# Input projection and first MLP matrix: the order of the last five products of a group

## The chip, the cores and the metric

The kernel runs on one core of a Trainium2 chip. The metric is the device time of one execution in microseconds (us), lower is better. The core's engines work side by side and wait for each other by semaphores: TensorE (PE, matmuls; PEld is its weight loading), VectorE (DVE), ScalarE (ACT), GpSimd (POOL) and SyncE (SP), which here only issues loads and stores. Matmuls write into PSUM, eight banks of 128 x 512 fp32; everything else lies in SBUF.

## The reference

One layer of a decoder trunk over 512 tokens of width 2048, in fp32:

```python
h = rmsnorm(x, g_mix[l])
z = jnp.einsum('bsd,dc->bsc', h, w_in[l])          # input projection, 10248 columns
cb, cc, cv, q, k, v, f_logit, gate_c, gate_a = jnp.split(z, SPLIT_POINTS, axis=-1)
...                                                # gated conv, forgetting attention, merge
x = x + jnp.einsum('bsd,de->bse', merged, w_mix_out[l])
h = rmsnorm(x, g_mlp[l])
u = jnp.square(jax.nn.relu(jnp.einsum('bsd,df->bsf', h, w_ff1[l])))   # first MLP matrix
x = x + jnp.einsum('bsf,fd->bsd', u, w_ff2[l])
...
return rmsnorm(x, g_final)
```

The change touches how the products with `w_in` and `w_ff1` are computed, and nothing of what they are.

## The kernel before

**Precision.** An fp32 operand is split in two: `split` (L100, L101) lets ACT write a rounded high half `hi` and DVE the rest, `lo`. A product is then hi·hi + hi·lo + lo·hi, three matmuls. The split weights lie in tiles th and tl, two buffers of each; so the split of a product can begin when the matmuls of the product before the last have read theirs.

**Seven products for eight.** Each group of columns of `w_in` or `w_ff1` is a two by two matrix of weight blocks X[i, j] (i: half of the rows, taken in steps of two; j: which of two column ranges). The tokens and rows on the activation side form a two by two matrix too, A11, A12, A21, A22. Instead of eight block products a group runs seven (Strassen's scheme in Winograd's form), with sums on both sides. On the activation side the sums S1 to S4 are made once per stage, already split (the tiles named A, S or ST). On the weight side they are made for each group, in place, by DVE (`sub`, L104):

- X00 becomes X01 - X00 (the first sum), used with S1
- X01 becomes X11 - X01 (the second), used with S3
- X11 becomes X11 - new X00 (the third), used with S2; the old X11 is used with S4
- X10 becomes X10 - new X11 (the fourth), used with A22

**A group.** `Group.head` loads X00 and X10 and runs A11 into bank a and A12 into bank b; `Group.tail` loads X01 and X11 (and X00 and X10 again if they were given up) and runs the other five. Bank a collects A11, S2 and S1, with a snapshot to SBUF by ACT after each (`snap`, L200). Bank c takes S4 alone, bank d S3 and then A22, with a snapshot of d between. Outputs leave through `put(i, j, ...)`: (0, 0) is a's first snapshot plus b; (1, 1) is the snapshot of d plus the last one of a; (0, 1) is the last snapshot of a plus c, read from the bank by `plus` (L217 where it is scaled, else L107); (1, 0) is a's second snapshot plus d. Each weight block lies in one of four slots (x0 to x3); `done` puts a slot at the end of the list `free`, and the next load takes the first of it, in the order X00, X10, X01, X11. SP issues the loads in this order, and a load waits until the slot's last reader is through.

A product of a group of width 256 (`mm_cols`, L139, L141 for the high half of the weights, L143 for the low half) has 48 matmuls of 128 x 256. Group gV0 and gV1 go through `mm_rows` (L156, L157, L159).

**The groups.** Input projection: gV0 and four groups `kq` run all their heads first and then all their tails, one tail behind the other; then gV1, six groups of conv columns and eight of gate columns follow whole, a head and then its tail (`whole`). Ahead of each of the first four conv groups, two heads of attention stand in the source. First MLP matrix (`ff1`): sixteen groups, of which 0 and 1 run head, head, tail, tail, and the others whole. The banks (a, b, c, d) of the heads held back are 6 for c and 7 for d in gV0 and all four kq groups, with a different a for each; c is bank 1 in all of ff1 but its last group, and bank 0 in the conv and gate groups.

In some groups (`apart`) S4 has two more small matmuls into a spare bank (L588): one conv group, three gate groups, and groups 2, 6, 10 and 14 of ff1.

**After ff1's outputs.** `put_u` applies a ReLU (L861), squares (L833, L838), makes sums of the four blocks of u for the next stage (into r, L850 for its low half) and stores high and low half to `s_d` by POOL's queue (L852, L853). The sums for j = 1 are made as soon as (0, 1) and (1, 1) are put; those for j = 0 wait in the list `later` until the next group's tail has taken its snapshot after S2.

**What sets the order.** The source's order is a priority: a planner walks it with its own costs, and on each engine takes the first instruction that it holds ready. So the order on an engine can differ from the source's where something is not ready, on DVE and ACT above all, and now and then on PE.

The stage after the input projection is `gemm_t` (L301), in the same banks; the one after ff1 is `unit`, whose banks come from a new pool, of which `a` overlaps banks 0 and 1 of the old.

Of the kernel before, what the change touches and what calls it, by code (L numbers as in the profile page):

```python
# [45 lines left out]
def tile_hybrid_block(ctx: ExitStack, tc, x, g_mix, w_in, b_f, b_gate, conv_w, w_conv_out,  # L46
# [56 lines left out]
    def sub(out, a, b):  # L103
        nc.vector.tensor_tensor(out=out, in0=a, in1=b, op=ALU.subtract)  # L104

    def add(out, a, b):
        nc.vector.tensor_tensor(out=out, in0=a, in1=b, op=ALU.add)  # L107
# [60 lines left out]
    class Group:  # L168
# [69 lines left out]
        def tail(self):  # L238
            if self.at:
                X = self.X  # L240
            else:
                X = {(i, 0): self.load(i, 0) for i in range(2)}
            X[0, 1], X[1, 1] = self.load(0, 1), self.load(1, 1)
            a = self.a
            c = self.acc("c")
            self.run(c, "S4", X[1, 1], True)
            sub(X[0, 0], X[0, 1], X[0, 0])
            sub(X[0, 1], X[1, 1], X[0, 1])
            sub(X[1, 1], X[1, 1], X[0, 0])
            self.run(a, "S2", X[1, 1], False)  # L250
            sub(X[1, 0], X[1, 0], X[1, 1])
            self.done(1, 1)
            s2 = self.snap(a)
            while later:
                later.pop(0)()
            d = self.acc("d")
            self.run(d, "S3", X[0, 1], True)
            self.done(0, 1)
            d1 = self.snap(d, self.scale)
            self.run(a, "S1", X[0, 0], False)  # L260
            self.done(0, 0)
            s4 = self.snap(a, self.scale)
            add(d1, d1, s4)
            self.put(1, 1, d1)
            self.plus(s4, c, self.scale)
            self.put(0, 1, s4)
            self.run(d, "A22", X[1, 0], False)
            self.done(1, 0)
            self.plus(s2, d)
            self.put(1, 0, s2)  # L270


    def eights(t, w=S):
# [804 lines left out]
```

## Time and profile before

| What | Value |
|---|---|
| Median of three runs | 2507.99 us (2504.74 to 2508.36) |
| The profiled execution, time | 2509.61 us |
| The profiled execution, span | 2507.9 us |
| Mean granted clock of TensorE | 0.996 |
| Weight loads of PE (PEld) | 90% of the span |
| DMA | 465.06 MB, mean 185 GB/s |

How to read it. The span is the time from the first to the last instruction of one profiled execution. In a timeline a row is start (us from the span's start), length (us), engine, line, operation, the tile written and the tiles read, and shapes; in brackets the idle time of the engine just before it and what ended it. In a view of waits a row is who waited for whom, then us in total, times, and the longest. In a view of windows a row is the stretch, its length, the busy time of PE, PEld, DVE, ACT and POOL with the number of instructions, the granted clock of PE, the busy share of the DMA engines and GB/s. Matmuls are pipelined: 0.28 us long, they start every 0.11 us or so, so the distance of starts tells the pace, not the length.

### The profile page before, as it was taken

To read this page: it belongs to the slowest core of one execution; us is meant where nothing else is said; L and a number is where in the kernel's file an instruction comes from. 1 tells how busy PE (TensorE), PEld (TensorE's weight loads), DVE (VectorE), ACT (ScalarE), POOL (GpSimd) and SP (SyncE) were. 2 spreads that over 40 slices of the span, in tenths; PEclk is the share of its full clock that TensorE was granted. 3 is DMA by queue.
4 is the path that set the end of the run, shared out by engine and by line. 5 is a ranking of instruction groups with operands and counts; after the bars stand their busy time and mean duration, and the time that the engine had idled before them with its cause. 6 is when DMAs were issued, how large, how long until landed. Compare 5 with 4: busy or idle time off the path is not lost. (4 is left out here: it accounts for less than half of the span.)

```text
span 2507.9 us, 39017 instructions
## 1 busy us (share of the span) xinstructions
PE 2453.0 (98%) x16911; PEld 2255.6 (90%) x16911; DVE 1902.2 (76%) x1498; ACT 1149.7 (46%) x1136; POOL 112.4 (4%) x184
## 2 busy tenths in 40 slices
PE   8999999999999999999999999999999999999997
PEld 7999989999999988888889999999998878787785
DVE  7877677789767744435678888898887877878888
ACT  6443434334444622235556666666664333333343
POOL 0000000000000000000000000000011000000010
PEclk9999999999999999999999999999999999999999
DMA  7554444456543554435654655646688557665573
GB/s 242 163 174 156 155 133 147 139 180 207 165 137 120 190 173 137 146 133 201 202 170 181 223 182 197 242 172 217 219 307 282 162 190 238 214 213 158 187 257 107
DMA packets 289919, 465.06 MB, mean 185 GB/s; under 512 B 10236, under 2 KB 194644, under 8 KB 289620
## 3 DMA queue, kind: packets, MB, share of 16 engines
q1 hardware_dynamic: 260704, 330.40, 41.2%
q0 software_dynamic: 28176, 131.08, 14.0%
q8 instruction: 132, 2.16, 0.4%
q10 hardware_dynamic: 868, 1.10, 0.1%
q14 instruction: 39, 0.32, 0.0%
HBM read 370.26 MB, written 92.27 MB: 184 GB/s over the span
## 5 line engine op out<-in xcount | busy, mean ns | idle before, releaser
L101 DVE TENSOR_TENSOR tl<-x,th 128x2048 fp32r<-128x2048 f32 (+1 forms) x252 | 574.7, 2288 | 216.6 <-ACT th L100 198.7
L100 ACT ACTIVATE th<-x 128x2048 fp32r<-128x2048 f32 (+1 forms) x252 | 482.4, 1917 | 498.5 <-PE a L141 184.8
L104 DVE TENSOR_TENSOR x<-x,x 128x2048 f32<-128x2048 f32 (+1 forms) x144 | 329.2, 2286 | 14.8 <-DMA x<-in_w_in_dram 7.1
L100 ACT ACTIVATE th<-y 128x2048 fp32r<-128x2048 f32 x80 | 153.7, 1921 | 271.3 <-DVE y L104 102.6
L101 DVE TENSOR_TENSOR tl<-y,th 128x2048 fp32r<-128x2048 f32 x80 | 182.8, 2284 | 47.3 <-ACT th L100 47.3
L101 DVE TENSOR_TENSOR tl<-raw,th 128x2048 fp32r<-128x2048 f32 x40 | 91.7, 2292 | 152.0 <-ACT th L100 151.5
L156 PE MATMUL a<-th,us 128*128 128x512 f32 x512 | 200.9, 392 | 3.0 <-ACT o L861 1.5
L157 PE MATMUL a<-th,us 128*128 128x512 f32 x512 | 199.4, 389 | 0.0
L139 PE MATMUL a<-ST,th 128*128 128x256 f32 x768 | 181.6, 281 | 5.9 <-ACT th L100 5.9
L141 PE MATMUL a<-ST,th 128*128 128x256 f32 x768 | 181.1, 280 | 0.0
L100 ACT ACTIVATE th<-raw 128x2048 fp32r<-128x2048 f32 x40 | 76.7, 1918 | 175.5 <-PE pt L302 62.6
L139 PEld LDWEIGHTS a<-ST,th 128*128 128x128 f32 x768 | 146.5, 191 | 6.6 <-ACT th L100 6.5
L141 PEld LDWEIGHTS a<-ST,th 128*128 128x128 f32 x768 | 146.5, 191 | 0.0
L139 PE MATMUL a<-S,th 128*128 128x256 f32 x576 | 134.1, 278 | 5.5 <-ACT th L100 5.5
L159 PE MATMUL a<-tl,us 128*128 128x512 f32 x512 | 136.9, 389 | 0.1
L141 PE MATMUL a<-S,th 128*128 128x256 f32 x576 | 133.5, 277 | 0.0
L156 PEld LDWEIGHTS a<-th,us 128*128 128x128 f32 x512 | 96.1, 188 | 28.5 <-ACT th L100 6.1
L139 PE MATMUL d<-ST,th 128*128 128x256 f32 x512 | 119.1, 278 | 0.0
L141 PE MATMUL d<-ST,th 128*128 128x256 f32 x512 | 119.1, 278 | 0.0
L159 PEld LDWEIGHTS a<-tl,us 128*128 128x128 f32 x512 | 96.0, 188 | 20.7 <-DVE tl L101 0.9
L139 PEld LDWEIGHTS a<-S,th 128*128 128x128 f32 x576 | 108.2, 188 | 6.8 <-ACT th L100 6.5
L157 PEld LDWEIGHTS a<-th,us 128*128 128x128 f32 x512 | 96.1, 188 | 19.6
(284 smaller groups left out, 6237.6 us busy)
## 6 DMA issues: line engine op xcount, KB each, us to landing
x<-in_w_in_dram SPq DMA_DIRECT2D x86, 1024.0 KB, 5.9
x<-in_w_ff_dram SPq DMA_DIRECT2D x66, 1024.0 KB, 7.8
y<-in_w_ff_dram SPq DMA_DIRECT2D x64, 1024.0 KB, 6.2
us<-s_d POOLq DMA_DIRECT2D x48, 1024.0 KB, 8.9
s_d<-rh POOLq DMA_DIRECT2D x32, 896.0 KB, 5.0
s_d<-r POOLq DMA_DIRECT2D x32, 896.0 KB, 8.2
raw<-in_w_mix_out_dram SPq DMA_DIRECT2D x24, 1024.0 KB, 5.1
g_d<-o SPq DMA_DIRECT2D x32, 256.0 KB, 2.2
```

Source lines behind the costliest of these rows:

```text
L100: nc.scalar.activation(out=hi, in_=src, func=AF.Copy)
L101: nc.vector.tensor_tensor(out=lo, in0=src, in1=hi.bitcast(F32), op=ALU.subtract)
L104: nc.vector.tensor_tensor(out=out, in0=a, in1=b, op=ALU.subtract)
L139: nc.tensor.matmul(o, hi[:, q, js], Sh, start=first and q == 0 and j == 0, stop=False, skip_group_check=True)
L141: nc.tensor.matmul(o, hi[:, q, js], Sl, start=False, stop=False, skip_group_check=True)
L156: nc.tensor.matmul(o, Sh, hi[:, q, :], start=begin and q == 0, stop=False, skip_group_check=True)
L157: nc.tensor.matmul(o, Sl, hi[:, q, :], start=False, stop=False, skip_group_check=True)
L159: nc.tensor.matmul(o, Sh, lo[:, q, :], start=False, stop=q == nq - 1, skip_group_check=True)
```

## The change

The five products of `Group.tail` run in the order S4, S3, S2, A22, S1 instead of S4, S2, S3, S1, A22. The first sum of weights stands ahead of S4, the second between S4 and S3, the third between S3 and S2, the fourth between S2 and A22. The snapshots, the calls of `done`, and the puts move with their products: the slots are given up in the order X01, X11, X10, X00 (before: X11, X01, X00, X10), and output (1, 0) is put ahead of (1, 1) and (0, 1). No instruction is added or removed.

```diff
             a = self.a
+            sub(X[0, 0], X[0, 1], X[0, 0])
             c = self.acc("c")
             self.run(c, "S4", X[1, 1], True)
-            sub(X[0, 0], X[0, 1], X[0, 0])
             sub(X[0, 1], X[1, 1], X[0, 1])
+            d = self.acc("d")
+            self.run(d, "S3", X[0, 1], True)
+            self.done(0, 1)
             sub(X[1, 1], X[1, 1], X[0, 0])
+            d1 = self.snap(d, self.scale)
             self.run(a, "S2", X[1, 1], False)
             sub(X[1, 0], X[1, 0], X[1, 1])
             self.done(1, 1)
             s2 = self.snap(a)
             while later:
                 later.pop(0)()
-            d = self.acc("d")
-            self.run(d, "S3", X[0, 1], True)
-            self.done(0, 1)
-            d1 = self.snap(d, self.scale)
+            self.run(d, "A22", X[1, 0], False)
+            self.done(1, 0)
             self.run(a, "S1", X[0, 0], False)
             self.done(0, 0)
+            self.plus(s2, d)
+            self.put(1, 0, s2)
             s4 = self.snap(a, self.scale)
             add(d1, d1, s4)
             self.put(1, 1, d1)
             self.plus(s4, c, self.scale)
             self.put(0, 1, s4)
-            self.run(d, "A22", X[1, 0], False)
-            self.done(1, 0)
-            self.plus(s2, d)
-            self.put(1, 0, s2)
```

## The prediction

> **What bounds the kernel now.** I read the page first, then the waits of TensorE, then the timelines around those waits.
>
> ```profile
> span 2507.9 us, 39017 instructions
> PE 2453.0 (98%) x16911; PEld 2255.6 (90%) x16911; DVE 1902.2 (76%) x1498; ACT 1149.7 (46%) x1136; POOL 112.4 (4%) x184
> ```
>
> TensorE (PE) is busy for 98% of the span, and the change removes none of its products. So it can only alter two things: how long PE stands still, and how fast it steps while it runs. The waits of PE, whole execution (us in total, times, longest):
>
> ```profile
> PE a L139 <- ACT th L100: 11.4, 8, 2.8
> PE d L156 <- ACT th L100: 8.1, 14, 3.7
> ...
> PE a L156 <- ACT o L861: 1.5, 1, 1.5
> PE a L156 <- ACT th L100: 0.8, 1, 0.8
> ...
> PE pt L301 <- DVE o L107: 0.4, 1, 0.4
> ```
>
> The d L156 row belongs to the last stage (`unit`), which is not touched. The eight waits of "a L139" and the one of "a L156" on th are all of one kind: the product that writes bank a behind one that writes bank c, which is S2 behind S4. Around one such group of the input projection (start us, length us):
>
> ```profile
> 140.69 0.28 PE L139 MATMUL d<-A,th 128*128 128x256 f32 x1
> 146.13 0.28 PE L139 MATMUL c<-S,th 128*128 128x256 f32 x1
> 152.66 0.39 PE L139 MATMUL a<-S,th 128*128 128x256 f32 x1 [0.92 <-ACT th L100]
> 152.88 0.28 PE L141 MATMUL a<-S,th 128*128 128x256 f32 x1
> ```
> ```profile
> 139.21 2.29 DVE L104 TENSOR_TENSOR x<-x,x 128x2048 f32<-128x2048 f32 x1 [1.33 <-DMA x<-in_w_in_dram]
> 141.53 0.69 DVE L107 TENSOR_TENSOR o<-o 128x512 f32<-128x512 f32 x1
> 142.25 0.69 DVE L217 SCALAR_TENSOR_TENSOR o<-c,o 128x512 f32<-128x512 f32 x1
> 143.28 2.29 DVE L104 TENSOR_TENSOR x<-x,x 128x2048 f32<-128x2048 f32 x1 [0.34 <-DMA x<-in_w_in_dram]
> 145.49 2.28 DVE L101 TENSOR_TENSOR tl<-x,th 128x2048 fp32r<-128x2048 f32 x1
> 147.69 0.68 DVE L107 TENSOR_TENSOR o<-d,o 128x512 f32<-128x512 f32 x1
> 148.29 4.61 DVE L104 TENSOR_TENSOR x<-x,x 128x2048 f32<-128x2048 f32 x2
> 152.82 2.29 DVE L101 TENSOR_TENSOR tl<-x,th 128x2048 fp32r<-128x2048 f32 x1
> ```
> ```profile
> 140.90 0.60 ACT L200 ACTIVATE o<-a 128x512 f32<-128x512 f32 x1 [4.84 <-PE a L143]
> 143.34 1.92 ACT L100 ACTIVATE th<-x 128x2048 fp32r<-128x2048 f32 x1 [1.84 <-DMA x<-in_w_in_dram]
> ```
>
> One product takes 5.44 us (140.69 to 146.13). S4's weights, the last of four loads, land at 143.3. From there VectorE (DVE) does the second sum, the low half of S4, a sum into an output, and only at 148.29 the third sum, on which S2 depends; ScalarE (ACT) then needs 1.92 us for S2's high half. S2 was due at 151.57 and starts at 152.66, 1.09 late. The rows of DVE also show that the first sum (139.21) stands ahead of S4's split (145.49) already, though the source has it behind: the planner starts what is ready. That part of the edit I cost at nothing, since the sum waits for its load either way.
>
> In most later groups of `ff1` the same chain just fits:
>
> ```profile
> 1723.34 1.93 ACT L100 ACTIVATE th<-x 128x2048 fp32r<-128x2048 f32 x1 [4.64 <-DVE x L104]
> 1726.29 0.28 PE L139 MATMUL a<-ST,th 128*128 128x256 f32 x1
> ```
>
> S2's high half is there at 1725.27 and S2 starts at 1726.29: 1.0 us to spare, PE never idle. Those groups have nothing to give.
>
> **What the waits cost beyond their length.** The longest one leaves a mark behind it:
>
> ```profile
> 1294.94 0.58 PE L139 MATMUL a<-ST,th 128*128 128x256 f32 x1 [2.85 <-ACT th L100]
> ...
> 1299.17 0.41 PE L141 MATMUL a<-ST,th 128*128 128x256 f32 x1
> 1299.38 0.41 PE L139 MATMUL a<-ST,th 128*128 128x256 f32 x1
> ...
> 1300.87 0.31 PE L141 MATMUL a<-ST,th 128*128 128x256 f32 x1
> ...
> 1338.95 0.38 PE L139 MATMUL a<-ST,th 128*128 128x256 f32 x1 [1.46 <-ACT th L100]
> ```
> ```profile
> 1286.00:1302.00 16.00, 13.15 (x91) 12.95 (x91) 15.43 (x12) 8.59 (x11) 1.15 (x2) 0.79 0.37 138
> ...
> 1342.00:1490.00 148.00, 148.00 (x1259) 148.00 (x1258) 125.63 (x96) 91.74 (x92) 7.99 (x15) 1.00 0.59 201
> 1500.00:1640.00 140.00, 140.00 (x1238) 140.00 (x1237) 120.80 (x93) 88.68 (x89) 7.45 (x14) 1.00 0.61 212
> ```
>
> After 2.85 us of idle the matmuls start 0.21 us apart instead of 0.113 until 1300.87, and the granted clock of that stretch is 0.79. The other two window rows show a second effect: PE is "busy" all the time in both, yet it starts a matmul every 117.6 ns in the first (148/1259) and every 113.1 ns in the second (140/1238), at the same granted clock. The slow stretch lies behind the restart at 1338.95, after 1.46 us of idle that left the clock at 1.00; it ends between 1490 and 1500, where group 6 runs its spare products (L588).
>
> **The change part by part.**
>
> 1. *S3 goes ahead of S2.* S3 needs the second sum only, S2 the third, A22 the fourth: one sum of 2.29 us per product of 5.44 us, instead of three ahead of one product. With the rows above, S3's high half can follow the second sum at 145.49 and be done at 147.5, against 151.57 when it is due: 4 us to spare. S2 then gets 5.44 us more. I take all nine waits as gone: 11.4 + 0.8 = 12.2 us idle. Each restart costs 0.28 on top: 1.09 late with 0.92 idle is 0.17, and the first step of 0.22 (152.66 to 152.88) is 0.11 over the normal one; nine times, 2.5. The slow clock behind the 2.85 wait: 5.93 us at 0.213 in place of 0.113 per step, 2.8. Together **-17.5 us**; bounds 0 and -17.5.
>
> 2. *The step of PE.* With no restart at 1338.95, group 2's own spare products should leave the fast step on: 1259 matmuls by 4.5 ns, **-5.6 us**. No row shows what a restart decides, so the bounds are 0 and -5.6.
>
> 3. *S1 goes last, so bank c comes free late.* c is read by L217 (`plus(s4, c)`), behind the snapshot of a after S1 and the add into d1. Before, S1 was followed by A22, 5.44 us of cover. Now the last product's end starts that chain, and where the next product is S4 of another group it must not write c before. This holds where tails follow tails: four boundaries among gV0 and the four kq groups (bank 6 for all), one between the two held heads of `ff1` (bank 1). Elsewhere two products of the next head lie between. The chain, by the rows: 140.90 to 142.94, 2.1 us, with both engines free. They may not be: DVE can be in S4's low half (145.49 to 147.69) and ACT in S3's high half; then the add starts about 148.0 and the bank is free near 149.4, 3.1 us idle. It can also be nothing, where PE has S3's matmuls to run meanwhile. Bounds 0 and 3.1 per boundary; I take 2.1, the chain as the trace shows it, plus 0.28: five times 2.4, **+11.9 us**. Behind PE nothing else queues there that is not waiting for PE itself.
>
> 4. *Ends of the two stages.* The hand-over to the last stage waits for the last reader of any bank:
>
> ```profile
> 1863.64 0.68 DVE L107 TENSOR_TENSOR o<-d,o 128x512 f32<-128x512 f32 x1
> ...
> 1864.42 0.47 PE L156 MATMUL a<-th,us 128*128 128x512 f32 x1 [1.47 <-ACT o L861]
> ```
>
> The wait is put down to an ACT row, but it ends 0.1 us behind the read of d (1863.64 + 0.68). That read has one link behind the last product; S1's has three, 2.1 us and up to 4.3 with a 2.28 sum in flight: +0.5 to +2.9, taken 1.5. The hand-over to `gemm_t` (0.4 idle now) has the same three links, but four banks to begin with: 0 to +1.7, taken 0.5. And the squares' sums of the last group (four adds of 0.42, one of 2.02: 3.7 us on DVE) move into the first unit: 0 to +3.7, taken 0.6. **+2.6 us**.
>
> 5. *Taken at nothing.* Bank d: its two uses and the snapshot between them keep one whole product of cover (S2 for S1), as has a (A22 for S3). The weight buffers are freed after the fourth to seventh product as before, so the SP queue's loads are issued at the same places; the stores of an output pair trade places. In `ff1` the pair of u-sums moves one product later, out of the last product into the head, with its two stores on POOL's queue and the reuse of r; their readers come a stage later. What hides this is DVE's slack (120.8 us busy of 140). If that cover were gone, ACT would wait for r with the next high half behind it; the bound is the 1.0 us to spare now, in 14 groups: 14 us. I exclude most of it because S2 no longer needs three sums early.
>
> Sum: -17.5 - 5.6 + 11.9 + 2.6 = **-8.6 us**, on the profiled execution's 2509.6 (span 2507.9) gives 2501.0. That execution lies 1.6 above the median of the runs, 2508.0; from the median the sum gives 2499.4. I say 2500.
>
> **Rivals.**
>
> *A, the step stays slow.* Only part 2 fails, because another restart (or none at all) leaves PE at 117.6 ns. For it: nothing in the trace says what picks the step, and the five new restarts are chances for the wrong one. Against: the group quoted at 140 steps at 113 ns (5.44 us for 48 matmuls) though waits of this kind stand in the groups around it. 2508.0 - 3.0 = 2505: within 0.2%.
>
> *B, bank c ends on the other side.* The chain of part 3, at the five boundaries, with busy engines: 3.1 us idle. That passes the 2.85 us after which the clock was seen to fall, so each boundary would cost 3.1 + 0.28 + 2.8 = 6.2, together 31; with part 2 lost as well, -17.5 + 31 + 2.6 = +16, 2524; with it, 2518. It decides from (17.5 + 5.6 - 2.6)/5 = 4.1 us per boundary, which an idle of 2.85 with its slow clock (5.9) exceeds and one of 2.1 does not. For it: the DVE and ACT rows at 145.5 fall just there. Against: waits of 1.5 us left the clock alone. The Trainium skill (TensorE: Matmul & The Clock Gate, "HAM oscillation") says that a gap over about 3.4 us puts the array back to half clock, by a window that runs freely; this trace shows it after 2.85, so the measurement is the stricter. By the page's figure B would need longer waits than I find.
>
> *C, PE fills the wait.* The planner puts S3's matmuls ahead of S4's, as it starts whatever is ready; part 3 falls to about 0.5 per boundary, 2.5 in all: -18.0, 2490. For it: the first sum standing ahead of S4's split is such a move. Against: S3's high half is itself only ready 1.3 us after the boundary (147.5 against 146.13).
>
> *D, the change doesn't do what it says.* If the planner's order of sums and splits were the same after it, the nine waits would stay and only parts of 3 appear: 2508, no change. Against: products write banks in source order, and the waits of step 1 hang on that order.
>
> **How the numbers follow.** Forecast 0.40, A 0.15, B 0.24, C 0.14, D 0.07. About 0.2%, 5 us, is what a measurement of this kernel can tell from no change. Faster by more: forecast and C, 0.54. Within: A and D, 0.22. Slower by more: B, 0.24. The range reaches down to C (2489) and up into B, to 2517, where some boundaries but not all trip the clock; the upper half of B and little else, about 0.15, is left out. The likeliest case has its own range, 2495 to 2504, from part 3 at 1.4 to 3.0 per boundary.
>
> **What would show it.** Step 1: no wait of "a" on th behind c, and S3 behind S4 with its high half early. Step 2: 1238 matmuls or so per 140 us right after group 2. Step 3: new waits of "c" on DVE's L217 or L107 at five places, about 2.1 us each, with the granted clock at 1.00 around them. Step 4: a wait of 2 to 4 us at the hand-over to the last stage. Step 5: no new wait in the groups of 1500 to 1860. I would be wrong if the waits at bank c were long enough to slow the clock, or if the groups that had none before got some.

## The result, and the profile after

The change makes the kernel slower: 2530.64 us median of six runs (2525.25 to 2535.30) beside 2508.18 of the kernel before on the same chip (2504.41 to 2511.37), a ratio of 1.0087, 95% interval 1.0072 to 1.0103. The prediction said 2500 with a range up to 2517; the time lies outside it, on the other side.

The head of the page after, then the waits of TensorE in the whole execution (us in total, times, longest):

```profile
span 2528.3 us, 39053 instructions
PE 2454.6 (97%) x16911; PEld 2251.9 (89%) x16911; DVE 1908.1 (75%) x1498; ACT 1150.5 (46%) x1136; POOL 112.6 (4%) x184
```
```profile
PE d L143 <- DVE tl L101: 20.7, 14, 2.4
PE d L156 <- ACT th L100: 8.7, 15, 3.7
PE d L139 <- ACT th L100: 8.3, 5, 2.5
...
PE d L159 <- DVE tl L101: 2.1, 2, 1.9
```

Each engine has as many instructions as before; the 36 more in the total of the head are none of theirs. The 1.6 us more of busy PE is noise beside a span 20.4 longer: PE stands still. The nine waits ahead of S2 are gone (the one wait of bank a on a split that is left, 0.7 us at 1316.66, is A11 of group 2 in ff1). In their place stand three kinds. Fourteen times the second half of S3 (L143, low half of the weights) waits for DVE's `split`: 20.7 us. Five times S3's first half waits for its high half: 8.3 us. And in the last stage two products wait for their low halves, 1.9 and 0.2 us.

The first matmul of each stage in the timeline of PE gives the length of the stages in the two profiled executions (us, one start less the other):

| Stage | before | after | difference |
|---|---|---|---|
| the five tails behind each other, to gV1 | 144.31 | 147.19 | +2.9 |
| gV1, conv and gate groups, to gemm_t | 645.88 | 644.25 | -1.6 |
| gemm_t to ff1 | 354.63 | 354.86 | +0.2 |
| ff1, groups 0 and 1 | 88.07 | 82.98 | -5.1 |
| ff1, group 2 to the last stage | 544.08 | 563.08 | +19.0 |
| last stage, to the end of PE | 630.59 | 635.83 | +5.2 |

So the loss is in ff1 from group 2 on, where the prediction had expected no new wait. One of these groups after, VectorE first, then the matmul that waits:

```profile
1717.06 2.29 DVE L104 TENSOR_TENSOR x<-x,x 128x2048 f32<-128x2048 f32 x1 [0.23 <-DMA x<-in_w_ff_dram]
1723.03 2.29 DVE L104 TENSOR_TENSOR x<-x,x 128x2048 f32<-128x2048 f32 x1 [3.67 <-DMA x<-in_w_ff_dram]
1725.23 0.69 DVE L107 TENSOR_TENSOR o<-o 128x512 f32<-128x512 f32 x1
1725.84 2.29 DVE L101 TENSOR_TENSOR tl<-x,th 128x2048 fp32r<-128x2048 f32 x1
...
1732.16 2.28 DVE L104 TENSOR_TENSOR x<-x,x 128x2048 f32<-128x2048 f32 x1
...
1734.69 2.29 DVE L104 TENSOR_TENSOR x<-x,x 128x2048 f32<-128x2048 f32 x1
1736.90 2.02 DVE L850 TENSOR_TENSOR r<-r,rh 128x1792 f32<-128x1792 f32 x1
...
1739.43 4.48 DVE L101 TENSOR_TENSOR tl<-x,th 128x2048 fp32r<-128x2048 f32 x2
```
```profile
1741.77 2.10 PE L143 MATMUL d<-ST,tl 128*128 128x256 f32 x16 [1.55 <-DVE tl L101]
```

The two rows at the top are the first and the second sum of weights. The second stands right behind the first in DVE's queue, and its operand X11 is still on its way: DVE is blocked for 3.67 us. Behind it wait things that were ready: the add into the output (1725.23; its operands were there at 1720.1, when ACT's snapshot of a ended) and the low half of A12 (1725.84). From 1723.03 on DVE runs with 0.2 us of idle, and the low half of S3, with the third and the fourth sum and L850 ahead of it, comes at 1739.43. PE, in S3 since 1736.29, is through with the high half first.

In the group quoted in the prediction, before, the same stretch of DVE reads so:

```profile
1707.68 2.28 DVE L104 TENSOR_TENSOR x<-x,x 128x2048 f32<-128x2048 f32 x1
...
1711.41 2.28 DVE L101 TENSOR_TENSOR tl<-x,th 128x2048 fp32r<-128x2048 f32 x1
...
1714.28 2.28 DVE L104 TENSOR_TENSOR x<-x,x 128x2048 f32<-128x2048 f32 x1
```

Six instructions stand between the first sum (1707.68) and the second (1714.28): the low half of A12 (1711.41) and, left out here, the reads of banks c and d and three sums of u. The second sum waits for nothing. Measured from the product A12 the second sum did not get later: it starts 2.0 us ahead of A12 after (A12 starts at 1724.98) and 1.1 us ahead before (1715.41). What changed is that the low half of A12, which was ready, stands behind it and not ahead of it. How large the difference is over most of groups 3 to 15, by the waits of DVE from 1350 to 1860, before and then after:

```profile
DVE tl L101 <- ACT th L100: 66.9, 38, 3.4
DVE x L104 <- DMA x<-in_w_ff_dram: 2.2, 3, 1.0
```
```profile
DVE x L104 <- DMA x<-in_w_ff_dram: 40.1, 25, 3.7
...
DVE tl L101 <- ACT th L100: 14.4, 25, 1.0
```

DVE's slack did not shrink much; it moved. Before, DVE was idle when it had nothing to do (it waited for the next split). After, it waits 40.1 us for loads: 23.1 in thirteen waits of the second sum, 17.0 in twelve of the first. That ready work stood behind the waiting sum is shown here for the one group alone. The Trainium skill (PSUM — Partial Sum Buffer, "Engine vs sequencer instructions") says that the queues of ScalarE, VectorE and GpSimd are strictly first in, first out; the rows at 1723.03 and 1725.23 agree.

### The profile page after: what moved, and what is told of

It is laid out like the page before. It is cut to its first block, busy times and chain, and to the rows that moved or that the text cites. A ratio compares the mean times of both kernels' runs of the same rounds, so it can differ in the third digit from the quotient of the medians.

```text
span 2528.3 us, 39053 instructions
## 1 busy us (share of the span) xinstructions
PE 2454.6 (97%) x16911; PEld 2251.9 (89%) x16911; DVE 1908.1 (75%) x1498; ACT 1150.5 (46%) x1136; POOL 112.6 (4%) x184
## 5 line engine op out<-in xcount | busy, mean ns | idle before, releaser
L139 PE MATMUL a<-ST,th 128*128 128x256 f32 x768 | 177.5, 277 | 0.7 <-ACT th L100 0.7
L141 PE MATMUL a<-ST,th 128*128 128x256 f32 x768 | 177.4, 277 | 0.0
L156 PE MATMUL d<-th,us 128*128 128x512 f32 x256 | 103.2, 403 | 8.7 <-ACT th L100 8.7
```

Source lines behind the costliest of these rows:

```text
L139: nc.tensor.matmul(o, hi[:, q, js], Sh, start=first and q == 0 and j == 0, stop=False, skip_group_check=True)
L141: nc.tensor.matmul(o, hi[:, q, js], Sl, start=False, stop=False, skip_group_check=True)
L156: nc.tensor.matmul(o, Sh, hi[:, q, :], start=begin and q == 0, stop=False, skip_group_check=True)
```

## The experiments

Theory **K**: the second sum at the head of DVE's queue, waiting for X11, costs the fourteen waits. Rival **U**: the u-sums of j = 1, which moved one product later into the head, overfill DVE between S1 and S3. First, in which part of the kernel is the loss? The new order in one part, the old in the other:

```diff
+        def tail(self):
+            if self.view is w_in:
+                self.tail_new()
+            else:
+                self.tail_old()
```

> New order in the input projection alone, the old one in the first MLP matrix. Both theories of the loss put it into the first MLP matrix, so: 2508 + 1, that is 2506 to 2512. The five tails that follow each other should cost 2.8 us more than before by the profile (gV1's first product at 234.6 against 231.8), the conv and gate groups 1 to 2 less. If the loss came from somewhere else than the groups of the first MLP matrix, this would be 2515 or more.

Measured: 2506.28 (ten runs) beside 2505.16 of before, ratio 1.0001 (0.9987 to 1.0016). In the tails that follow each other the new order lost 3.4 us (147.67 for 144.31), and it won back 2.8 in the groups behind them. With `w_ff1` in the condition instead:

> The other half: new order in the first MLP matrix alone. Both theories: 2526 to 2532, with 14 waits of the products into bank d on a low half in DVE, 1.5 us each, and the first unit of the last stage 5 us longer.

Measured: 2527.07 (four runs), ratio 1.0083 (1.0068 to 1.0098). The loss is ff1's. Now K against U: the second sum alone is held back on DVE, by an order without a semaphore, behind the previous group's read of bank c and the low half of A12; the u-sums stay where the change put them.

```diff
-            sub(X[0, 1], X[1, 1], X[0, 1])
+            i = sub(X[0, 1], X[1, 1], X[0, 1])
+            if self.view is w_ff1 and self.cs[0] >= 2 * S:
+                behind(i, read_c[-1], self.low["A12"])
```

> New order everywhere; in groups 2 to 15 of the first MLP matrix the second sum of weights is issued on DVE behind the read of bank c of the group before and behind the low half of A12, so that it no longer stands idle at the head of DVE's queue waiting for X11's load (3.1 to 3.7 us a group, 40 us in all). Theory K (the queue: DVE blocked by that wait makes S3's low half late): the 14 waits on the low half vanish, 2508 to 2514. Theory U (the u-sums of j = 1, now between S1 and S3, fill the window whatever the order): waits of 1 us or more stay in most groups, 2522 to 2532.

Measured: 2506.47 (ten runs), ratio 1.0009 (0.9996 to 1.0021): 1.3 us above the kernel before on the same chip, where the kernel after was 22.5 above. All of ff1 takes 622.75 us in place of 646.06. The same place in a group of this kernel:

```profile
1704.19 2.29 DVE L101 TENSOR_TENSOR tl<-x,th 128x2048 fp32r<-128x2048 f32 x1 [0.29 <-ACT th L100]
...
1707.12 0.69 DVE L112 TENSOR_TENSOR o<-c,o 128x512 f32<-128x512 f32 x1
1707.73 2.28 DVE L104 TENSOR_TENSOR x<-x,x 128x2048 f32<-128x2048 f32 x1
...
1718.53 2.28 DVE L101 TENSOR_TENSOR tl<-x,th 128x2048 fp32r<-128x2048 f32 x1
1720.73 2.28 DVE L104 TENSOR_TENSOR x<-x,x 128x2048 f32<-128x2048 f32 x1
```

The low half of A12 and the two adds (one left out here) go first, the sum waits for nothing, and of the fourteen waits of S3 one is left: 1.6 us in group 2, where neither sum waits for a load in the kernel after either, so that K does not account for it. K's forecast came true but for that one; U, with its u-sums untouched, does not hold. DVE's wait for loads in 1340 to 1850 is down to 4.5 us. But one edit moved more than one sum: the planner now sets the low half of S3 (1718.53) ahead of the fourth sum (1720.73), which the kernel after has the other way round (1739.43 and 1734.69). A third edit left the second sum alone and held the fourth back behind the low half of S3:

```diff
-            sub(X[1, 0], X[1, 0], X[1, 1])
+            i = sub(X[1, 0], X[1, 0], X[1, 1])
+            if self.view is w_ff1 and self.cs[0] >= 2 * S:
+                behind(i, self.low["S3"])
```

> New order everywhere; in groups 2 to 15 of the first MLP matrix the fourth sum (2.29 us, used only by A22) is issued behind the low half of S3 instead of ahead of it. DVE stays blocked for X11's load. Both theories would see S3's low half 2.3 us or more earlier, which covers lateness of 1.5 to 2.7: most of the 14 waits go, 2510 to 2517. If it goes to 2514 or lower, the order of sum and low half on DVE is enough by itself to explain the loss; if 1 us a group stays, 2522 or more, the window is too full or the block decides.

Measured: 2559.57 (four runs), ratio 1.0210 (1.0191 to 1.0229), against both theories. S3's waits are gone but for the one of group 2, although DVE still waits 28.0 us for loads from 1350 to 1860, some 20 of it ahead of the second sum; A22 waits instead. So a blocked second sum does not make S3 late by itself: the low half of S3 has to stand behind the fourth sum and L850 as well. In the group shown above S3's low half was 1.55 us late, beside a block of 3.67 us and a fourth sum of 2.29; by these rows, to take away either would do, which is an estimate. No run takes the block away and leaves the fourth sum where it was. The waits of PE in 1350 to 1900, and ACT and PE in one group:

```profile
PE d L144 <- ACT o L205: 31.0, 12, 5.2
```
```profile
1727.98 0.63 ACT L846 ACTIVATE r<-c 128x512 f32<-128x512 f32 x1 [4.11 <-DMA s_d<-r]
1728.52 0.58 ACT L205 ACTIVATE o<-d 128x512 f32<-128x512 f32 x1
```
```profile
1729.15 0.38 PE L144 MATMUL d<-ST,th 128*128 128x256 f32 x1 [2.42 <-ACT o L205]
```

With the fourth sum late, the planner sets the first u-sum of j = 0 (r<-c) ahead of the snapshot of bank d on ACT. That u-sum rewrites r, of which there is one buffer, and r's last store is still under way: ACT is blocked for 4.11 us, the snapshot behind it is late, and A22 may not write d. It is a blocked head of a queue once more, on another engine and with a store in the place of a load.

Next, the parts of the prediction that spoke of gains. The new order in groups 0 and 1 of ff1 alone (the condition of the first experiment with `self.view is w_ff1 and self.cs[0] < 2 * S`):

> The new order in groups 0 and 1 of ff1 alone, where two tails follow each other; all else as before. Theory K (the loss is the second sum at the head of DVE's queue, in the groups that run whole): none of the 14 waits of S3 on its low half; the waits of 2.85 us (with its slow clock) and of 1.46 us ahead of S2 go, one of up to 1.9 us ahead of S3 comes at the boundary between the two tails: 2499 to 2504. If the fast step also follows in group 2: 2496 to 2499. Rival U (any use of the new order in ff1 puts the u-sums in the way): at least two waits of S3, 2506 to 2510.

Measured: 2502.90 (twelve runs) beside 2505.85, ratio 0.9986 (0.9975 to 0.9998). No wait of S3 on its low half: the rival falls. The wait ahead of S2 in group 2, 1.46 us before, did not go: that group is in the old order, and the wait is longer (the matmul as the timeline of PE has it):

```profile
1335.40 0.38 PE L139 MATMUL a<-ST,th 128*128 128x256 f32 x1 [2.36 <-ACT th L100]
```

Then bank c, with two banks in turn (3 is free once the heads are through), the new order in the input projection only:

```diff
-    heads = [gV0] + [kq(hp, ((a,), (3,), (6,), (7,))) for hp, a in enumerate((0, 1, 2, 5))]
+    heads = [gV0] + [kq(hp, ((a,), (3,), (3 if hp % 2 == 0 else 6,), (7,))) for hp, a in enumerate((0, 1, 2, 5))]
```

> The new order in the input projection alone, with bank c taken in turn from banks 6 and 3 in the tails that follow each other. Theory (part 3 of the prediction: the waits at the four boundaries come from the one bank c, for which TensorE runs S3 ahead of S4): S4 ahead of S3 again, none of the four waits of S3 on its high half (5.3 us in all with the new order alone); 2499 to 2502 beside 2506 of the new order in the input projection with one bank. Rival (S3's high half is late by itself, whatever the bank): the same waits, or as long ones, ahead of S3 or S2; 2505 to 2508.

Measured: 2495.50 (six runs), ratio 0.9952 (0.9937 to 0.9968), better than expected. The waits of PE from 85 to 250, after and then with two banks:

```profile
PE d L139 <- ACT th L100: 6.4, 4, 2.5
...
```
```profile
PE c L159 <- DVE tl L101: 0.3, 1, 0.3
```

S4 stands ahead of S3 again and the four waits are gone; the five tails take 137.91 us, 9.8 less than with the new order and one bank (some 1.7 of it, an estimate, is the clock, which stood at 0.50 for 3.41 us behind one wait of the latter). The rest of the input projection is 0.5 shorter. So the one bank was nearly the whole price of the new order there.

The last stage. The kernel after loses 5.2 us there, all in the first unit: S3's high half 0.6 late, its low half 1.9, and behind that a slow clock (0.50 from 1891.24 to 1894.65; the row is in the last section). The rows of PE:

```profile
1885.97 0.50 PE L156 MATMUL d<-th,us 128*128 128x512 f32 x1 [0.59 <-ACT th L100]
1890.00 1.19 PE L159 MATMUL d<-tl,us 128*128 128x512 f32 x4 [1.92 <-DVE tl L101]
```

Three tries. The last group in the old order, on top of the late second sum:

```diff
+            if self.view is not w_ff1 or self.cs[0] < DFF - S:
+                self.tail_new()
+            else:
+                self.tail_old()
```

> The kernel after, with the second sum of groups 2 to 14 behind the read of bank c and the low half of A12, and the last group of ff1 in the order of before. Theory (the first unit of the last stage loses 5 us since the u-sums of the last group move into it with S1's output): the first unit runs as before, with a wait of 1 to 2 us at the hand-over; 2501 to 2504, 3 to 5 less than with the new order in the last group (2506.5). Rival (the first unit is late for another reason, its own loads or splits): 2506 to 2508, the waits in the first unit stay.

Measured: 2511.77 (twelve runs), ratio 1.0018 (1.0007 to 1.0030), above its expected range and no better than with the new order there (1.0009, on another chip; the intervals overlap). The first unit did get better (last stage 632.20 for 635.09), but ff1 with the hand-over got 9.2 longer (631.98 for 622.75), 7.8 of it a wait at the hand-over. At the seam of the two orders the sums of j = 1 of group 14 come late and those of group 15 early, and ACT waits for r's stores twice (ACT's waits, 1838 to 1870):

```profile
ACT r L886 <- DMA s_d<-r: 6.6, 1, 6.6
ACT r L881 <- DMA s_d<-r: 5.9, 1, 5.9
```

Second, the u-sums of j = 1 of the last group left out, on the kernel after:

> The kernel after, without the sums and splits of u for j = 1 in the last group of ff1 (their place in the store is filled with the sums of j = 0). Theory (they fill DVE and ACT in the first unit of the last stage): from the first product of the last stage to the end 630 to 632 us, as before, in place of 635.8; 2524 to 2527. Rival (the second sum of the first unit waits for its load at the head of DVE's queue, as in the groups of ff1, whatever the u-sums): 634 to 636; 2529 to 2532.

Measured: 2533.50 (four runs), ratio 1.0120 (1.0101 to 1.0139), and the last stage takes 638.87 us. Theory and rival both said less. With j = 1 gone, the sums of j = 0 moved forward in ACT's and DVE's queues, to a place where the store of r was not done, and S3 began 4.8 us late:

```profile
1880.11 0.63 ACT L840 ACTIVATE r<-c 128x512 f32<-128x512 f32 x1 [4.45 <-DMA s_d<-r]
```
```profile
1889.82 0.80 PE L156 MATMUL d<-th,us 128*128 128x512 f32 x1 [4.82 <-ACT th L100]
```

Less arithmetic, a later first unit: in this run it counted for more what stood at the head of DVE's and ACT's queues than how much they had to do.

Third, the combinations. All three repairs at once, with the last group in the old order:

> The three repairs together: the new order with the second sum late in groups 2 to 14, the order of before in the last group, and two banks in turn for c where tails follow tails (input projection and groups 0 and 1 of ff1). If each loss is what theory K and part 3 say, they add: 2506.5 less 4 (first unit) less 7 (five boundaries) = 2494 to 2498, faster than both kernels. Rival: the gains take each other's place (a wait moves on to the next product or the next load): 2500 to 2506.

Measured: 2501.14 (twelve runs), ratio 0.9980 (0.9969 to 0.9992). The hand-over (4.9 us of idle) eats most of it. The new order only in the input projection and in groups 0 and 1, with two banks:

> The new order where tails follow tails and in the rest of the input projection, that is in gV0 to the last gate group and in groups 0 and 1 of ff1, with two banks in turn for c; the order of before in groups 2 to 15. If the parts add as their stages did when run alone (the input projection's tails 9.7 us shorter than before, ff1 8.3 shorter with one bank and some 2 more with two, the last stage as before): 2486 to 2490. Rival (the two gains share a cause, such as the pace after a restart): 2492 to 2498.

Measured: 2496.84 (twelve runs), ratio 0.9977 (0.9963 to 0.9991) beside 2504.29. The gains did not add: waits stand now ahead of S2 in group 2 (3.2 us) and of A12 in group 3 (2.5 us), and the clock fell behind both. The new order everywhere, second sum late, two banks:

> The new order everywhere, with the second sum late in groups 2 to 15, and two banks in turn for c in the tails that follow each other. If part 3 adds to the repair of the second sum: 2506.5 less 11 (the input projection) less 2 (ff1's first boundary): 2491 to 2496, with the first unit of the last stage still 5 us late. Rival (the new order in the groups that run whole is worth as much as it costs in the first unit): no more than 2 us from the kernel that keeps the order of before there.

Measured: 2496.95 (twelve runs), ratio 0.9971 (0.9960 to 0.9983), 1 us above its range and within 0.2 us of the kernel just before (2496.84, same chip), as the rival had said. Beside that kernel ff1 is 9.2 us shorter (622.74 for 631.97), the last stage 6.0 longer (635.81 for 629.76), and the five tails, the same code in both, 3.8 longer (141.21 for 137.44; see the two paces in the last section). What is left to win is the first unit. There S2's high half stood on ACT behind the rounding of r, which waited for the u-sums on DVE:

```profile
1855.63 1.71 ACT L857 ACTIVATE rh<-r 128x1792 fp32r<-128x1792 f32 x1 [2.38 <-DVE r L104]
1857.24 1.89 ACT L100 ACTIVATE th<-t 128x2048 fp32r<-128x2048 f32 x1
```

The last edit, on top of that kernel, puts the last group's u-sums behind the low half of S2 in the first unit (`between` runs after S2, and the pool of r closes after the first unit):

```diff
         run(a, "S2", t2, False)
+        between()
...
+            i = add(r[:, 4, :], low[:, 0, :], r[:, 3, :])
+            if low_s2:
+                behind(i, low_s2[0])
```

> The new order everywhere with the second sum late and two banks in turn for c, and the last group's sums of u (j = 1, then j = 0) behind the low half of S2 in the first unit of the last stage. Theory (in the first unit S2's high half stands in ScalarE's queue behind the rounding of r, which waits for the u-sums on VectorE, and later a high half behind the wait for r's store; S3's low half is late by 1.4 us for other sums): the 2.1 us ahead of S2 go, and perhaps the 1.9 us later on: the last stage 631 to 634 us in place of 635.8, 2492 to 2495. Rival (S2 waits for its sum, or its other operand, from a load that is late by itself): 635 to 637 and 2496 to 2499.

Measured: 2488.31 (six runs, 2487.57 to 2495.80) beside 2505.27, ratio 0.9934 (0.9919 to 0.9950): faster than before, and the lowest median of all, though its interval overlaps that of the two banks in the input projection alone (0.9937 to 0.9968). All that PE waits for between 1848 and 1905, and the split that was late:

```profile
PE d L164 <- DVE tl L101: 1.4, 1, 1.4
```
```profile
1858.08 1.90 ACT L100 ACTIVATE th<-t 128x2048 fp32r<-128x2048 f32 x1
...
1867.36 1.68 ACT L861 ACTIVATE rh<-r 128x1792 fp32r<-128x1792 f32 x1
```

S2's high half (1858.08) now precedes the rounding of r (1867.36), and the last stage takes 631.21 us, 4.6 less. The medians, on two chips, differ by 8.6; the other 4 us are not accounted for (the profiled execution, 2495.80, is the slowest of the six, and its five tails went at the slow pace almost throughout).

## Why the prediction was wrong, point by point

**Step 1, nine waits gone (-17.5).** Right in kind. S3 needs only the second sum, and none of the nine waits is left. Groups 0 and 1 of ff1, where the longest one stood, are 5.1 us shorter with the new wait at their boundary counted in. In the input projection the gain was there too, but under the waits of step 3 until these were taken away.

**Step 2, the pace of PE (-5.6).** Right behind group 2, wrong as a lasting gain. From 1341 the products of the kernel after stand 5.44 us apart where they do not wait. But the slow step came back later in ff1, as in this window, where 336 matmuls with 0.4 us of idle took 40 us, 117.9 ns each:

```profile
1700.00:1740.00 40.00, 39.62 (x336) 39.62 (x336) 32.51 (x26) 23.81 (x24) 2.13 (x4) 1.00 0.54 186
```

Over all of ff1 some 1,680 steps were at the slow pace before and some 750 after; at 4.5 ns each the difference is 4.2 us, an estimate, of the 5.6.

**Step 3, bank c (+11.9).** Near in size, but by luck; wrong in kind. Rival C's move came true: PE ran S3 ahead of S4 at all five boundaries. But S3's high half was 1.3 to 2.5 us late (8.3 in all), where C had priced 0.5. The four boundaries of the input projection took back the 5.5 us of waits that stood there before (four of bank a, 4.7 in all, and the one of 0.8 us) and 2.9 more, 8.4 in all, and two banks gave back 9.8 us. The chain of 2.1 us that I priced was not what a product S4 would have met. At the boundary of 145.5 us the read of c came at 151.97, behind two low halves, an add (left out here) and a sum on DVE, so that c came free 7 us behind the boundary:

```profile
144.76 4.49 DVE L101 TENSOR_TENSOR tl<-x,th 128x2048 fp32r<-128x2048 f32 x2
...
149.77 2.28 DVE L104 TENSOR_TENSOR x<-x,x 128x2048 f32<-128x2048 f32 x1
151.97 0.68 DVE L217 SCALAR_TENSOR_TENSOR o<-c,o 128x512 f32<-128x512 f32 x1
```

**Step 4, ends of stages (+2.6).** The hand-over to the last stage, +1.5, did not come: PE goes on with the first unit at 1879.74 without a gap, while the last read of c is still to come:

```profile
1874.58 0.69 DVE L107 TENSOR_TENSOR o<-d,o 128x512 f32<-128x512 f32 x1 [1.07 <-PE d L143]
...
1886.69 0.68 DVE L107 TENSOR_TENSOR o<-c,o 128x512 f32<-128x512 f32 x1
```

So it did not wait for "the last reader of any bank"; the read of d, at whose end the wait of before stopped, is now 4.5 us ahead of it. The hand-over to `gemm_t`, taken at 0.5, did not show either: the wait of 0.4 that stood there is gone, and the stage is 0.2 longer. The first unit, taken at 0.6, cost 5.2 (the experiments end in removing 4.6 of it).

**Step 5, "taken at nothing".** This is the step that failed. It said that in ff1 DVE's slack hides what moves, bounded the loss at 14 us and excluded "most of it because S2 no longer needs three sums early". The fourteen waits of S3 cost 20.7 us. The slack was there, but an engine that takes its work in order can lose its slack in one place: the second sum, ahead of everything that was ready, blocked it 3.67 us in the group shown, and the low half of S3 stood behind the fourth sum and L850, which S3 does not need. The same work in another order left no such wait in thirteen of the fourteen groups; how the blame divides between the block and what stood ahead of the low half stays open, and so does the wait of group 2. The prediction had the sign for it in hand, the row of 139.21 with 1.33 us of wait for a load, and read it as "the sum waits for its load either way". It asked what the sum waits for, and not what waits behind the sum. Why the planner put it there is argued only: the outputs' adds come one product later in the new order, so DVE had nothing else ready when the planner's own costs had X11 landed; the chip had it later.

**The rivals.** B's clock drop did not come in the profiled execution of the kernel after. It did come at one boundary of the input projection in each of the five other profiled kernels with the new order and one bank there, for 3.41 us at a clock of 0.50: some 1.7 us, an estimate, where B had 31 in all. The length of 2.85 us that B took for the limit is not one (last section). C's order came, at more than three times its price (8.3 us for 2.5). The range reached up to 2517 for bank c alone; no rival ended in the groups without a wait, which the last part of the prediction named as the way to be wrong.

## What to carry to other kernels

Before a reorder, look on each engine that works in order for the instructions that wait for a DMA (a load, or a store that holds a buffer) and ask what stands behind them; an average slack of 20% need not hide what is queued behind such a head. After a reorder, compare an engine's idle time by what ended it: the same idle time with "DMA" in the place of "nothing to do" is the mark of it. A wait that is removed at the boundary of two groups may need a second bank or buffer before it pays, and where two orders meet, the seam can cost more than either.

## What the runs showed of the hardware

**Two paces in the same code.** Groups of the input projection that are alike in the kernel before and in the one with the new order in groups 0 and 1 of ff1 alone, from 212 to 229 us, before and then the other:

```profile
212.00:229.00 17.00, 17.00 (x152) 17.00 (x151) 9.42 (x6) 7.25 (x6) 0.00 (x0) 1.00 0.80 252
```
```profile
212.00:229.00 17.00, 17.00 (x147) 17.00 (x146) 8.88 (x6) 7.45 (x6) 0.00 (x0) 1.00 0.81 252
```

152 matmuls beside 147, no idle time, the same granted clock: one and the same code steps at either pace. A restart can set it: in the timeline of PE after, of the twenty restarts behind 0.9 us or more without a start (the five tails and ff1), seventeen went on at 113 ns and three, at 117.82, 176.84 and 1580.46, at 118. But the pace also changes without one: behind each of the four restarts in the tails it turned over at the end of the first product, twice from 118 to 113 and twice back. What decides between them no run shows. It is worth some us an execution: with the new order and two banks the same code of the five tails took 137.4 to 137.9 us where some 220 of its 1,180 steps were slow, 141.2 with some 950 and 141.8 with nearly all. It may be one reason why parts measured alone did not add to the microsecond.

**The clock and the place of a wait.** In the kernel before, 2.85 us of idle brought the clock down. In the kernel after, the wait of 2.5 us and all fourteen in S3 (up to 2.4) left it alone, and in the first unit one of 1.92 brought it down. So length alone does not decide. The record of the granted clock shows what does. It changes only on a grid of 3.41 us: in the kernel after it fell at 1891.24 and at 2478.34, and these 587.10 us are 172 steps of 3.4133. Windows on that grid, in the kernel after around the waits of 2.5 and of 1.92 us, then in the one with the new order in the input projection alone, around the same boundary:

```profile
112.90:116.31 3.41, 2.39 (x22) 2.19 (x20) 2.86 (x2) 2.37 (x2) 0.00 (x0) 1.00 0.12 41
116.31:119.73 3.42, 1.91 (x16) 1.91 (x17) 3.42 (x2) 1.94 (x2) 0.00 (x0) 1.00 0.00 0
...
1887.83:1891.24 3.41, 1.49 (x7) 1.05 (x6) 3.21 (x4) 1.00 (x3) 0.00 (x0) 1.00 1.01 387
1891.24:1894.65 3.41, 3.41 (x9) 2.64 (x8) 1.76 (x1) 3.41 (x3) 0.56 (x1) 0.50 1.02 386
```
```profile
115.57:118.98 3.41, 1.44 (x12) 1.44 (x13) 3.41 (x2) 2.40 (x2) 0.00 (x0) 1.00 0.00 0
118.98:122.39 3.41, 3.41 (x18) 3.41 (x18) 3.41 (x3) 0.00 (x0) 0.00 (x0) 0.50 0.34 76
```

The wait of 2.5 us is cut by the grid, with 1.0 us of idle in one window and 1.5 in the next, and the clock stays. The one of 1.92 us lies whole in one window, and the clock is at 0.50 in the next. At the same boundary a wait of 2.7 us put 1.97 of its idle into one window, and the clock fell. Over the fourteen profiled executions, from 60 us on, there are 9,946 such windows that began at the full clock. None of the 9,901 with less than 1.8 us of idle was followed by a fall, each of the 38 with 1.95 or more was, and of the seven between them four were. So what counts is how much idle falls into one window, and by this count a wait of 2 to 3.5 us can go either way by where it lies. The Trainium skill (TensorE: Matmul & The Clock Gate, "What's actually happening") tells of a window of 3413 ns that runs freely, and of a fall to half the clock after an idle window of that length. The trace agrees with the window and the half; but here some 1.9 us of idle in one window was enough, and the measurement decides.
